# Zero rows under the low-part score pass and the Fourier tail of a two-layer encoder, with three scratch tiles merged

## The chip, the cores and the metric

One Trainium2 chip, one of its cores. The metric is the device time of one execution in microseconds, the median of several runs. The engines named below are TensorE (PE in the rows, its weight loads PEld), VectorE (DVE), ScalarE (ACT), GpSimd (POOL) and SyncE (SP, which issues most DMAs).

## What is computed

Two layers over 1040 positions (1024 and 16 meta tokens) of width 1024, all in float32:

```python
for li in range(DEPTH):                       # 2
    h = rms_norm(h_res, norm_gain[li])
    f_in, q, k, v, gate = split(h @ w_in[li])
    f_out = fourier_mixer(f_in, w_fourier[li])   # Re(FFT2 over positions, 128 channels), 4 groups, linear map
    q, k = rotary(rms_norm(q)), rotary(rms_norm(k))   # 4 heads x 2 maps x 64
    p = softmax(q k^T / 8)                     # two maps per head
    o = rms_norm((p[0] - lam * p[1]) @ v) * (1 - lambda_init)
    h_res = h_res + (concat(f_out, o) * silu(gate)) @ w_out[li]
return h_res[:, 16:]
```

## The kernel before

**Products in three passes.** Every large matrix product is made of float32r parts: each operand is split in a high and a low part, and high by high, high by low and low by high are added up in PSUM. TensorE takes at most 512 columns in a matmul, and the operands' rows (the contracted dimension) are the partitions, up to 128 of them.

**Order of work.** A layer has a Fourier part (`fourier`), the projection of head 0 (`head_projection`), attention (`attention`) and the output projection. The projections of heads 1 to 3 and the Fourier half of the output projection are a generator that `fill(n)` advances by some steps, of three matmuls of 512 columns each, between the steps of attention. The order on each engine is fixed when the program is built: a planner simulates the program's timeline and puts each instruction where its inputs and buffers are ready by its own reckoning, with priorities for what frees a PSUM bank. At run time each engine takes its instructions in that order.

**Attention.** A head's queries are handled in groups of two token tiles of 128 rows (in layer 0 the last group also has the 16 meta rows). One tile of one group is an item: 36 items in layer 0, 32 in layer 1. `scores` (line 620) handles an item in two passes, one for each of the two maps c. A pass takes the one large PSUM tile S (three banks), and makes three matmuls of 264, 512 and 264 columns with the high part of the queries against 128 rows, 64 of high and 64 of low keys (line 630), then three more with the low part of the queries against the 64 rows of high keys (line 632). VectorE finds the row maximum and copies S out (line 637), ScalarE takes the exponential (line 640). After both passes VectorE joins the two maps (line 648). One item later `drain` transposes the result in eight and one matmuls (`transposes`, lines 658 and 665), and after the last tile of a group `values` multiplies it with the values (lines 677 and 678, the latter with 80 rows). `finish` (line 683) is called in the gap after the first score pass of the second item of the next group: it transposes the group's output `osb` into a PSUM bank `pb` (line 691), copies it to `ot` (693), squares it on ScalarE for the norm, with the squares going to the scratch tile `sqo` and only the sum used (699), and multiplies with the gate (706).

**Queries.** `build_queries` (line 602) makes for each group `qa` and `qb`, each with 128 rows, and one `ql` whose upper and lower 64 rows are the low parts for the two maps. A pass of `scores` reads the half of `ql` and the half of the keys that belong to its map.

**Banks.** PSUM has the tile S, two banks G for the projections (`gbank`) and three banks M (`bank`) that are handed out in turn to transposes, keys, queries, values, `finish` and the Fourier transform.

**Fourier part.** `transform` (line 358) is called four times in a layer, for one channel group each: it folds 1040 positions to four sequences of about 260, of which 256 are multiplied with tables in `tab` (line 391, six matmuls for each sequence) and the remaining 4 or 5 are packed with their low parts into 48 rows of `tl`, transposed to `ut` and multiplied with the 48-row table `tabt` (line 393, one matmul for each sequence). That is 16 matmuls of line 393 in a layer. Both tables are loaded by DMA from GpSimd's queue (lines 317 and 319).

**Head projection.** For each token tile 24 matmuls of 512 columns (line 546), then `evacuate`: ScalarE makes the gate's tanh in `thg` (line 479, one buffer), VectorE the gate in `gs` (481, two buffers), which SyncE writes to DRAM (487); ScalarE copies the rest out of the bank (482 to 485). Scratch tiles under the tag `sq` have three buffers of 288 columns, which `rope_tables` and `small_constants` use as well.

Of the kernel before, what the change touches and what calls it, by code (L numbers as in the profile page):

```python
# [10 lines left out]
F32 = mybir.dt.float32  # L11
# [7 lines left out]
P = 128  # L19
# [14 lines left out]

C0 = 248                                    # first score column, so that the chunks end at bank edges
CHUNKS = ((0, 264), (264, 776), (776, 1040))
# token columns of each pass of the Fourier projections, per layer
FCHUNKS = (((0, 256), (256, 640), (640, 1040)), ((384, 768), (0, 384), (768, 1040)))
HOME = "G0G1G2G0G"                          # psum bank of each token tile while head 0 is projected
# weight splits given to the vector engine: every n-th one (0: none)  # L40
SHF, SH0, SHH, SHO = 2, 4, (3, 3, 0, 2), 2
STAGE = 4                                   # token tile at which the next weights start to load
WAT, MT = 2, 6                              # token tiles after which the first weights and the meta tile come
EVAC = 600                                  # priority of what frees a psum bank
# pace of the projections that run between the steps of attention, per layer
FIRST, FILL, LAG, XHD = (8, 5), (0.96, 0.93), (7, 8), (0, 1)
KEYS = (2, 1)                               # query group from which the next head's keys are built


@with_exitstack  # L50
def trunk(ctx: ExitStack, tc, x, meta, ngain, w_in, w_f, qg, kg, lq1, lk1, lq2, lk2, subg, w_out,
# [15 lines left out]
    def nm(s):  # L67
        uid[0] += 1
        return f"{s}_{uid[0]}"
# [10 lines left out]
    def f(ap):  # L80
        return ap.bitcast(F32)

# [1 line left out]
    ident = cst.tile([P, P], F32, name="ident")  # L84
# [35 lines left out]
    def small_constants(ini):  # L120
        W = DEPTH * HD
        lv = [ini.tile([P, 288], F32, tag="sq", name=nm("lv"), bufs=3) for _ in range(2)]
        for i, v in enumerate((lq1, lk1, lq2, lk2)):
# [20 lines left out]

    def rope_tables(li, rp):
        cs = rp.tile([P, 288], F32, tag="sq", name=nm("cs"), bufs=3).rearrange("p (j t d) -> p j t d", j=2, d=ROT)
        sp.dma_start(cs, rope_d)
        gb = rp.tile([P, 288], F32, tag="sq", name=nm("gb"), bufs=3)[:, 0:64]
        gb = gb.rearrange("p (i j d) -> p i j d", i=2, j=2)
        for i, g in enumerate((qg, kg)):  # L150
            sp.dma_start(gb[:, i, 0, :], g[li, 0:ROT].partition_broadcast(P))
            sp.dma_start(gb[:, i, 1, 0:8], g[li, 8:16].partition_broadcast(P))
            sp.dma_start(gb[:, i, 1, 8:16], g[li, 0:8].partition_broadcast(P))
        for j, dst in enumerate((cgt, sgt)):
            for i in range(2):
                dve.tensor_tensor(dst[:, :, i, :], cs[:, j],
                                  gb[:, i, j, :].unsqueeze(1).to_broadcast([P, NT + 1, ROT]), op=ALU.mult)

# [1 line left out]
    class Weights:  # L160
# [50 lines left out]

# [1 line left out]
    def norm_tile(hT, hM, gb, xt, t, wk, inplace=False):  # L213
# [24 lines left out]

# [1 line left out]
    def token_tiles(li):  # L240
# [60 lines left out]

# [1 line left out]
    def fourier(li, hT, fo, ep, w, nxt):  # L303
# [10 lines left out]
        ul = fo.tile([P, 8, P], F32R, name="ul")  # L314
        ut = fo.tile([48, P], F32R, name="ut")
        tab = fo.tile([P, 4, 2, 2, NFT], F32R, name="tab")
        pool.dma_start(tab, dft_d)
        tabt = fo.tile([48, 4, NFT], F32R, name="tabt")
        pool.dma_start(tabt, dftt_d)
        ph = fo.tile([P, 4, NFT], F32R, name="ph")  # L320
# [37 lines left out]
        def transform(g, usb):  # L358
# [24 lines left out]
            pe.transpose(pb[0:48, 0:P], tl, ident)  # L383
            act.copy(ut, pb[0:48, 0:P])
            dve.tensor_tensor(ut[32:48], pb[32:48, 0:P], f(ut[32:48]), op=sub)
# [32 lines left out]
        for gp in range(2):  # L418
# [20 lines left out]
            if gp == 0:  # L439
                channel_maps()  # L440
                with tc.issue_after(ins.ins):
                    rope_tables(li, ep)
                    if li == 0:
                        small_constants(ep)
# [7 lines left out]

# [1 line left out]
    def head_projection(li, h, hT, hM, ep, wk, store, w, nxt, progress):  # L454
# [9 lines left out]
        def evacuate(t, ps, a, kv):  # L464
            nonlocal ss
            R = tile_rows(t)
            with tc.high_priority(EVAC):
                if t == NT:
                    pm = [ep.tile([P, 288], F32, tag="sq", name=nm("pm"), bufs=3) for _ in range(2)]
                    for part, u, v in ((pm[0], a, 256), (pm[1], 256, 384 if kv else 512)):  # L470
                        part = part[0:R, u % 256:(v - 1) % 256 + 1]
                        act.copy(part, ps[32:32 + R, u:v])
                        dve.tensor_tensor(part, ps[0:R, u:v], part, op=ALU.add)
                    pqk, pvg = pm[0], pm[1]
                else:
                    pqk, pvg = ps[:, 0:256], ps[:, 256:512]
                if not kv:
                    th = ep.tile([P, P], F32, tag="thg", name=nm("thg"), bufs=1)
                    act.activation(th[0:R], pvg[0:R, P:2 * P], AF.Tanh, scale=0.5)
                    gs = ep.tile([P, P], F32, tag="gs", name=nm("gs"), bufs=2)  # L480
                    dve.scalar_tensor_tensor(gs[0:R], th[0:R], 1.0, pvg[0:R, P:2 * P], op0=ALU.add, op1=ALU.mult)
                act.copy(qk[0:R, t, a:256], pqk[0:R, a:256])
                sq = ep.tile([P, 288], F32, tag="sq", name=nm("sq"), bufs=3)
                act.activation(sq[0:R, a:256], pqk[0:R, a:256], AF.Square)
                act.copy(va[0:R, t, :], pvg[0:R, 0:P])  # L485
# [9 lines left out]
            if t % 3 == 2:  # L495
# [12 lines left out]

                r1 = ep.tile([P, 288], F32, tag="sq", name=nm("r1"), bufs=3)
                r2 = ep.tile([P, 288], F32, tag="sq", name=nm("r2"), bufs=3)  # L510
                r1 = r1[:, 0:12 * ROT].rearrange("p (t c d) -> p t c d", t=6, c=2)
# [41 lines left out]

# [1 line left out]
    def attention(li, wk, store, fill, marks, ready, progress):  # L555
# [5 lines left out]
        pool.memset(f(att), 0.0)  # L561
        half = (slice(0, HD), slice(HD, P))

        def group_tiles(gi):
# [37 lines left out]
        def build_queries(h, gi):  # L602
# [8 lines left out]
            qb = wk.tile([P, 272], F32R, tag="qb", name=nm("qb"))  # L611
            ql = wk.tile([P, 272], F32R, tag="ql", name=nm("ql"))
            for dst, s, o in ((qa, half[0], half[1]), (qb, half[1], half[0])):
                act.activation(dst[s, 0:w], pb[s, 0:w], AF.Copy, scale=qgc[s, li:li + 1])
                dve.tensor_copy(dst[o, 0:w], f(dst[s, 0:w]))
                dve.scalar_tensor_tensor(ql[s, 0:w], pb[s, 0:w], qgc[s, li:li + 1], f(dst[s, 0:w]),
                                         op0=ALU.mult, op1=ALU.subtract)
            return qa, qb, ql

        def scores(keys, gq, i, t, ls, gaps):  # L620
            R = tile_rows(t)
            qo = P * i
            ql = gq[2]
            l2 = sm.tile([P, 1], F32, tag="l2", name=nm("l2"))
            pp = []
            for c in range(2):
                q, kk, s = gq[c], keys[c], half[c]
                ps = big()
                for a, b in CHUNKS:
                    pe.matmul(ps[0:R, C0 + a:C0 + b], lhsT=q[:, qo:qo + R], rhs=kk[:, a:b], start=True, stop=False)  # L630
                for a, b in CHUNKS:
                    ins = pe.matmul(ps[0:R, C0 + a:C0 + b], lhsT=ql[s, qo:qo + R], rhs=kk[s, a:b],  # L632
                                    start=False, stop=True)
# [49 lines left out]
        def finish(h, gi, osb, ls):  # L683
            sets = [(0, 2, P)] + ([(2, 1, NMETA)] if len(group_tiles(gi)) > 2 else [])
            for i0, n, R in sets:
# [4 lines left out]
                for i in range(n):  # L690
                    pe.transpose(pb[0:R, P * i:P * i + P], osb[:, P * (i0 + i):P * (i0 + i) + R], ident)
                ot = wk.tile([P, 2, P], F32, tag="ot", name=nm("ot"), bufs=1)
                act.copy(ot[0:R, 0:n], pb[0:R, 0:P * n].rearrange("p (t d) -> p t d", t=n))
                r1 = sm.tile([P, 2], F32, tag="r1", name=nm("r1"))
                dve.reciprocal(r1[0:R, 0:n], ls[0:R, i0:i0 + n])
                so = sm.tile([P, 2], F32, tag="so", name=nm("so"))
                sqo = wk.tile([P, P], F32, tag="sqo", name=nm("sqo"), bufs=1)
                for i in range(n):
                    act.activation(sqo[0:R], ot[0:R, i], AF.Square, scale=r1[0:R, i:i + 1],
                                   accum_out=so[0:R, i:i + 1])  # L700
# [63 lines left out]

# [1 line left out]
    def phase_out(li, nh, gb, wk, w, load, ready):  # L766
# [52 lines left out]

# [1 line left out]
    def open_pool(name, side=None, bufs=1):  # L821
# [175 lines left out]
```

## Time and profile before

| | |
|---|---|
| median of 3 runs | 1269.27 us (1268.62 to 1269.63) |
| span of the profiled execution | 1267.7 us |
| busy, TensorE / VectorE / ScalarE / GpSimd | 1224.9 / 838.8 / 646.9 / 258.7 us |
| granted clock of TensorE, mean share | 0.993 |
| line 630 and line 632, matmuls | 408 each |
| line 393, matmuls | 32 |
| attention stretches | about 224 to 603 and 861 to 1219 us |

The times are of one execution, the span from its first to its last instruction. A group's busy time is the time in which at least one of its instructions was under way. Matmuls are pipelined, so that each one's duration (0.28 us for 256 columns) is longer than the distance to the next start; what a matmul costs in a dense stream is read from the starts. A timeline row gives start, time until the end, engine, line and operation, output and inputs, sizes as rows\*columns of the weights and partitions x columns of the moving operand, the count that is merged in the row, and in brackets the idle time of the engine before it with what ended it. "issue" is a wait for which the profile shows no cause.

### The profile page before, as it was taken

Reading aid. Unit: us, or ns where it says so; the run is one execution under the profiler, and the core shown is the slowest. Engines: PE = TensorE matmul, PEld = TensorE weight load, DVE = VectorE, ACT = ScalarE, POOL = GpSimd, SP = SyncE. Lnnn points to the kernel's source line nnn. Section 1 sums busy time; section 2 is a strip of 40 time slices with the busy share of each in tenths; the row PEclk is TensorE's granted clock in tenths of the full one; section 3 lists DMA queues with packets and bytes.
Section 4 is the critical chain, followed back from the end, with each engine's and each line's share of the span. In section 5 each row is a group of like instructions: output and inputs, shape, how many; then the busy total and the mean of one; then the engine's idle time right before and its main releaser. Section 6 shows DMA issues by size and latency. Waiting matters only on the chain.

```text
span 1267.7 us, 18708 instructions
## 1 busy us (share of the span) xinstructions
PE 1224.9 (97%) x6676; PEld 999.5 (79%) x6676; DVE 838.8 (66%) x1793; ACT 646.9 (51%) x1588; POOL 258.7 (20%) x219
## 2 busy tenths in 40 slices
PE   6999899999999999999999999999999999999998
PEld 6999787777776776778879998877777877777786
DVE  6352435777788778888673425458687887788863
ACT  6232325566656667556453222345566676756631
POOL 5101215023112112102011103160141122211200
PEclk9999899999999999999999999999999999999999
DMA  7320203003002004643335202020020110364353
GB/s 229 121 72 34 71 26 96 7 16 87 12 23 75 15 24 151 206 151 125 129 112 169 67 18 84 28 78 26 17 80 24 46 49 24 95 212 149 108 154 117
DMA packets 103612, 105.46 MB, mean 83 GB/s; under 512 B 11232, under 2 KB 87584, under 8 KB 103264
## 3 DMA queue, kind: packets, MB, share of 16 engines
q1 hardware_dynamic: 103104, 99.59, 25.0%
q0 software_dynamic: 416, 4.70, 1.1%
q8 instruction: 52, 0.85, 0.3%
q14 instruction: 40, 0.33, 0.1%
HBM read 74.62 MB, written 29.62 MB: 82 GB/s over the span
## 4 chain that ended last, share of the span: by engine, by line
PE 75%; DVE 8%; DMA 5%; ACT 4%; issue 4%; POOL 2%; SPq 1%; POOLq 0%; ACTq 0%; DVEq 0%
PE G L546 23%; PE G L286 10%; PE G L350 6%; PE M L677 6%; PE S L350 6%; PE S L632 6%; PE S L630 4%; PE S L546 3%; PE M L658 3%; PE M L391 2%; DMA wst<-in_w_in_dram 2%; POOL wl L184 2%; DVE p L637 1%; DVE p L648 1%; PE M L402 1%
## 5 line engine op out<-in xcount | busy, mean ns | idle before, releaser
L546 PE MATMUL G<-wh,hT 128*128 128x512 f32 x896 | 313.6, 409 | 4.2 <-ACT va L485 1.8
L546 PEld LDWEIGHTS G<-wh,hT 128*128 128x128 f32 x896 | 168.1, 189 | 57.2 <-issue 16.1
L640 ACT ACTIVATE p<-p,mx 128x1040 f32<-128x1040 f32 x136 | 158.5, 1165 | 101.7 <-DVE p L637 101.1
L637 DVE TENSOR_SCALAR_CACHE_REDUCE p<-S 128x1040 f32<-128x1040 f32 x136 | 167.9, 1234 | 45.9 <-PE S L632 34.1
L546 PE MATMUL G<-wl,hT 128*128 128x512 f32 x448 | 177.6, 398 | 1.6 <-POOL wl L184 1.5
L184 POOL TENSOR_TENSOR wl<-wst,wh 128x512 fp32r<-128x512 f32 x82 | 114.4, 1405 | 254.3 <-ACT wh L182 167.3
L286 PE MATMUL G<-wh,yh 128*128 128x512 f32 (+2 forms) x276 | 109.5, 409 | 3.7 <-DVE xt L293 2.7
L286 PE MATMUL G<-wl,yh 128*128 128x512 f32 (+2 forms) x276 | 106.5, 395 | 0.0
L182 ACT CAST wh<-wst 128x512 fp32r<-128x512 f32 x128 | 74.6, 619 | 56.6 <-DMA wst<-in_w_in_dram 24.2
L632 PE MATMUL S<-k,ql 64*128 64x264 f32 (+3 forms) x408 | 99.7, 350 | 0.0
L546 PEld LDWEIGHTS G<-wl,hT 128*128 128x128 f32 x448 | 84.8, 189 | 19.0 <-POOL wl L184 3.2
L500 POOL TENSOR_TENSOR rsq<-ss,nhalf 128x12 f32<-128x12 f32 x24 | 55.0, 2292 | 218.0 <-DVE ss L498 194.1
L350 PE MATMUL G<-hT,wh 128*128 128x384 f32 (+3 forms) x384 | 96.6, 332 | 0.0
L286 PE MATMUL G<-wh,yl 128*128 128x512 f32 (+1 forms) x260 | 94.1, 402 | 0.0
L663 DVE TENSOR_TENSOR atl<-M,ath 128x512 fp32r<-128x512 f32 x136 | 86.5, 656 | 9.6 <-ACT ath L662 8.5
L350 PE MATMUL S<-hT,wh 128*128 128x256 f32 (+3 forms) x384 | 91.4, 321 | 1.0 <-DVE sg L438 1.0
L648 DVE SCALAR_TENSOR_TENSOR p<-p,cc,p 128x1040 f32<-128x1040 f32 (+1 forms) x68 | 90.2, 1327 | 1.4
L662 ACT CAST ath<-M 128x512 fp32r<-128x512 f32 x136 | 73.0, 562 | 23.5 <-PE M L658 22.8
L632 PEld LDWEIGHTS S<-k,ql 64*128 64x128 f32 (+1 forms) x408 | 55.0, 179 | 35.1 <-issue 34.2
L184 DVE TENSOR_TENSOR wl<-wst,wh 128x512 fp32r<-128x512 f32 x46 | 46.6, 1017 | 43.5 <-ACT wh L182 43.4
L658 PE MATMUL M<-ident,p 128*128 128x128 f32 x544 | 73.5, 271 | 0.9 <-DVE atl L663 0.4
L703 POOL TENSOR_TENSOR rso<-so,nhalf 128x2 f32<-128x2 f32 (+1 forms) x36 | 26.8, 746 | 229.3 <-DVE so L701 223.5
(190 smaller groups left out, 2554.5 us busy)
## 6 DMA issues: line engine op xcount, KB each, us to landing
wst<-in_w_in_dram SPq DMA_DIRECT2D x64, 192.0 KB, 2.8
xt<-in_x_dram SPq DMA_DIRECT2D x16, 512.0 KB, 4.2
wst<-in_w_in_dram SPq DMA_DIRECT2D x32, 256.0 KB, 3.6
wst<-in_w_out_dram SPq DMA_DIRECT2D x16, 512.0 KB, 4.0
xmid<-xt SPq DMA_DIRECT2D x16, 512.0 KB, 3.3
xt<-xmid SPq DMA_DIRECT2D x16, 512.0 KB, 4.4
tab<-in_dft_dram POOLq DMA_DIRECT2D x2, 2096.0 KB, 10.6
yfd<-sg SPq DMA_DIRECT2D x8, 520.0 KB, 2.7
```

What stands on the lines that cost most here:

```text
L182: act.copy(h, self.staged[q][:, j, :])
L184: eng.tensor_tensor(l, self.staged[q][:, j, :], f(h), op=ALU.subtract)
L286: pe.matmul(pb[0:m, 0:e - c], lhsT=a[:, k, 0:m], rhs=b[2 * k + n][:, c:e], start=k == 0 and i == 0, stop=k == 3 and i == n_pass - 1)
L350: pe.matmul(o, lhsT=w[k][:, c:c + P], rhs=hT[:, k, s, a:b], start=k == 0 and i == 0, stop=k == KT - 1 and i == 2)
L546: pe.matmul(pss[t][0:part.shape[-1], a:b], lhsT=part, rhs=w[k][:, a:b], start=k == 0 and i == 0, stop=k == KT - 1 and i == len(pairs) - 1)
L632: ins = pe.matmul(ps[0:R, C0 + a:C0 + b], lhsT=ql[s, qo:qo + R], rhs=kk[s, a:b], start=False, stop=True)
L637: dve.tensor_scalar(pc[0:R], ps[0:R, C0:C0 + L], -1.0, None, op0=ALU.mult, op1=ALU.min, accum_out=mx[0:R])
L640: act.activation(pc[0:R], pc[0:R], AF.Exp, bias=mx[0:R], scale=-1.0, accum_out=lc)
L648: dve.scalar_tensor_tensor(pp[0][0:R], pp[1][0:R], cc[0:R], pp[0][0:R], op0=ALU.mult, op1=ALU.add)
L658: pe.transpose(pb[:, R * j:R * j + R], pa[0:R, P * kt:P * kt + P], ident[0:R, 0:R])
L663: dve.tensor_tensor(atl[:, 4 * c:4 * c + 4, qo:qo + R], src, f(hi), op=ALU.subtract)
L677: pe.matmul(po[:, 0:w], lhsT=v[:, kt, :], rhs=a[:, kt, 0:w], start=kt == 0 and i == 0, stop=False)
```

## The change

The low part of the queries gets four tiles of its own that live as long as `attention`, two for each map, with zeros written once in the 64 rows that the map doesn't use; the matmuls of line 632 take all 128 rows of them and of the keys. `ut` and `tabt` get 128 rows, zeroed before their 48 rows are filled, and line 393 takes all of them. `thg` is merged into `gs`, `ot` into the first 256 columns of `osb`, and the squares go back to the PSUM bank `pb` in place of `sqo`. `cs` of the rotary tables leaves the tag `sq` for a tile of its own in the Fourier part's pool, and the other tiles under `sq` become 256 columns wide. The rest of the diff takes comments away.

```diff
-        cs = rp.tile([P, 288], F32, tag="sq", name=nm("cs"), bufs=3).rearrange("p (j t d) -> p j t d", j=2, d=ROT)
+        cs = rc.tile([P, 288], F32, name=nm("cs")).rearrange("p (j t d) -> p j t d", j=2, d=ROT)
...
-        ut = fo.tile([48, P], F32R, name="ut")
+        ut = fo.tile([P, P], F32R, name="ut")
+        pool.memset(f(ut), 0.0)
         tab = fo.tile([P, 4, 2, 2, NFT], F32R, name="tab")
         pool.dma_start(tab, dft_d)
-        tabt = fo.tile([48, 4, NFT], F32R, name="tabt")
-        pool.dma_start(tabt, dftt_d)
+        tabt = fo.tile([P, 4, NFT], F32R, name="tabt")
+        pool.memset(f(tabt), 0.0)
+        pool.dma_start(tabt[0:48], dftt_d)
...
-            act.copy(ut, pb[0:48, 0:P])
+            act.copy(ut[0:48], pb[0:48, 0:P])
...
-                    th = ep.tile([P, P], F32, tag="thg", name=nm("thg"), bufs=1)
-                    act.activation(th[0:R], pvg[0:R, P:2 * P], AF.Tanh, scale=0.5)
                     gs = ep.tile([P, P], F32, tag="gs", name=nm("gs"), bufs=2)
-                    dve.scalar_tensor_tensor(gs[0:R], th[0:R], 1.0, pvg[0:R, P:2 * P], op0=ALU.add, op1=ALU.mult)
+                    act.activation(gs[0:R], pvg[0:R, P:2 * P], AF.Tanh, scale=0.5)
+                    dve.scalar_tensor_tensor(gs[0:R], gs[0:R], 1.0, pvg[0:R, P:2 * P], op0=ALU.add, op1=ALU.mult)
...
+        qlow = [[wk.tile([P, 272], F32R, name=f"ql{n}{c}", bufs=1) for c in range(2)] for n in range(2)]
+        for pair in qlow:
+            for c in range(2):
+                pool.memset(f(pair[c][half[1 - c]]), 0.0)
...
-            ql = wk.tile([P, 272], F32R, tag="ql", name=nm("ql"))
-            for dst, s, o in ((qa, half[0], half[1]), (qb, half[1], half[0])):
+            low = qlow[gi % 2]
+            for dst, ql, s, o in ((qa, low[0], half[0], half[1]), (qb, low[1], half[1], half[0])):
...
-                    ins = pe.matmul(ps[0:R, C0 + a:C0 + b], lhsT=ql[s, qo:qo + R], rhs=kk[s, a:b],
+                    ins = pe.matmul(ps[0:R, C0 + a:C0 + b], lhsT=ql[:, qo:qo + R], rhs=kk[:, a:b],
                                     start=False, stop=True)
...
-                ot = wk.tile([P, 2, P], F32, tag="ot", name=nm("ot"), bufs=1)
+                ot = osb[:, 0:2 * P].rearrange("p (t d) -> p t d", t=2)
...
-                sqo = wk.tile([P, P], F32, tag="sqo", name=nm("sqo"), bufs=1)
                 for i in range(n):
-                    act.activation(sqo[0:R], ot[0:R, i], AF.Square, scale=r1[0:R, i:i + 1],
+                    act.activation(pb[0:R, P * i:P * i + P], ot[0:R, i], AF.Square, scale=r1[0:R, i:i + 1],
                                    accum_out=so[0:R, i:i + 1])
```

## Rows read from the trace of the kernel before

**Rows 1.** The page: busy time by engine, then the chain's shares.

```profile
PE 1224.9 (97%) x6676; PEld 999.5 (79%) x6676; DVE 838.8 (66%) x1793; ACT 646.9 (51%) x1588; POOL 258.7 (20%) x219
...
PE 75%; DVE 8%; DMA 5%; ACT 4%; issue 4%; POOL 2%; SPq 1%; POOLq 0%; ACTq 0%; DVEq 0%
```

**Rows 2.** Attention stretches: length, busy PE, PEld, DVE, ACT, POOL, clock, DMA.

```profile
224.00:603.00 379.00, 369.85 (x1999) 283.81 (x1998) 300.80 (x664) 238.79 (x584) 70.25 (x59) 1.00 0.24 75
861.00:1219.00 358.00, 353.15 (x1924) 279.07 (x1922) 288.29 (x609) 220.51 (x535) 69.06 (x54) 1.00 0.25 78
```

**Rows 3.** Timeline of TensorE's matmuls around one score pass.

```profile
401.92 0.29 PE L630 MATMUL S<-k,qb 128*128 128x264 f32 x1
402.04 0.28 PE L678 MATMUL M<-att,vt 80*128 80x256 f32 x1
402.16 0.52 PE L630 MATMUL S<-k,qb 128*128 128x512 f32 x2
402.61 0.74 PE L632 MATMUL S<-k,ql 64*128 64x264 f32 x3
403.27 0.50 PE L546 MATMUL G<-wh,hT 128*128 128x512 f32 x1
403.61 0.39 PE L546 MATMUL G<-wl,hT 128*128 128x512 f32 x1
403.84 0.63 PE L546 MATMUL G<-wh,hT 128*128 128x512 f32 x2
```

**Rows 4.** Timeline of TensorE's weight loads around the same pass.

```profile
402.04 0.31 PEld L630 LDWEIGHTS S<-k,qb 128*128 128x128 f32 x2
402.61 0.41 PEld L632 LDWEIGHTS S<-k,ql 64*128 64x128 f32 x3 [0.25 <-issue]
```

**Rows 5.** Line 632: weight loads (ns min/median/max), idle time before it (us, times).

```profile
L632 PEld LDWEIGHTS S<-k,ql x408: 88/185/188, 225.1 to 1218.8; 64*128 64x128 f32 x128, 64*16 64x16 f32 x8
...
  issue: 34.2, 133
```

**Rows 6.** Timeline around a matmul of line 393; then that line's count.

```profile
84.76 0.28 PE L391 MATMUL M<-tab,ul 128*128 128x262 f32 x1
84.97 0.38 PE L393 MATMUL M<-tabt,ut 48*128 48x262 f32 x1
85.28 0.51 PE L391 MATMUL M<-tab,uh 128*128 128x260 f32 x2
85.62 0.28 PE L391 MATMUL M<-tab,ul 128*128 128x260 f32 x1
...
L393 PE MATMUL M<-tabt,ut x32: 381/382/387, 85.0 to 825.6; 48*128 48x262 f32 x16, 48*128 48x260 f32 x16
```

**Rows 7.** Stretches from item to item, as rows 2: first and last of 66.

```profile
224.50:231.50 7.00, 6.46 (x29) 4.43 (x28) 3.60 (x8) 2.64 (x6) 0.00 (x0) 1.00 0.00 0
...
1199.40:1211.40 12.00, 12.00 (x61) 9.34 (x60) 11.67 (x24) 7.42 (x19) 0.70 (x1) 1.00 0.27 81
```

**Rows 8.** Timeline around one `finish`; then waits of line 665: us, times, longest.

```profile
259.66 0.35 ACT L693 COPY ot<-M 128x256 f32<-128x256 f32 x1
...
261.79 0.40 ACT L699 ACTIVATE sqo<-ot,r 128x128 f32<-128x128 f32 x1
...
260.87 0.28 PE L665 MATMUL M<-ident,p 128*16 128x128 f32 x1
...
PE M L665 <- DVE atl L663: 4.3, 6, 1.1
```

**Rows 9.** Timeline of GpSimd as attention begins; then line 319's DMA issues.

```profile
206.31 0.33 POOL L561 MEMSET att<- 80x272 f32 x1
...
209.84 2.38 POOL L595 TENSOR_TENSOR vl<-va,vh 128x1024 fp32r<-128x1024 f32 x1 [2.95 <-ACT vh L594]
...
L319 POOL DMA_DIRECT2D tabt<-in_dftt_dram x2: 522/524/527, 38.2 to 674.2; - x2
```

**Rows 10.** Line 487, the gate's write-out: issue to landing.

```profile
DMA to landing us min/median/max: 1.3/1.5/4.1
```

More of the change, by code (lines that the diff above doesn't have):

```diff
@@ L121, in small_constants @@
         W = DEPTH * HD
-        lv = [ini.tile([P, 288], F32, tag="sq", name=nm("lv"), bufs=3) for _ in range(2)]
+        lv = [ini.tile([P, 256], F32, tag="sq", name=nm("lv"), bufs=3) for _ in range(2)]
         for i, v in enumerate((lq1, lk1, lq2, lk2)):
@@ L143, in small_constants, with rope_tables @@
                               op0=ALU.mult, op1=ALU.mult)
-    def rope_tables(li, rp):
-        cs = rp.tile([P, 288], F32, tag="sq", name=nm("cs"), bufs=3).rearrange("p (j t d) -> p j t d", j=2, d=ROT)
+    def rope_tables(li, rp, rc):
+        cs = rc.tile([P, 288], F32, name=nm("cs")).rearrange("p (j t d) -> p j t d", j=2, d=ROT)
         sp.dma_start(cs, rope_d)
-        gb = rp.tile([P, 288], F32, tag="sq", name=nm("gb"), bufs=3)[:, 0:64]
+        gb = rp.tile([P, 256], F32, tag="sq", name=nm("gb"), bufs=3)[:, 0:64]
         gb = gb.rearrange("p (i j d) -> p i j d", i=2, j=2)
@@ L441, in fourier @@
                 with tc.issue_after(ins.ins):
-                    rope_tables(li, ep)
+                    rope_tables(li, ep, fo)
                     if li == 0:
@@ L468, in evacuate @@
                 if t == NT:
-                    pm = [ep.tile([P, 288], F32, tag="sq", name=nm("pm"), bufs=3) for _ in range(2)]
+                    pm = [ep.tile([P, 256], F32, tag="sq", name=nm("pm"), bufs=3) for _ in range(2)]
                     for part, u, v in ((pm[0], a, 256), (pm[1], 256, 384 if kv else 512)):
@@ L477, in evacuate @@
                 if not kv:
-                    th = ep.tile([P, P], F32, tag="thg", name=nm("thg"), bufs=1)
-                    act.activation(th[0:R], pvg[0:R, P:2 * P], AF.Tanh, scale=0.5)
                     gs = ep.tile([P, P], F32, tag="gs", name=nm("gs"), bufs=2)
-                    dve.scalar_tensor_tensor(gs[0:R], th[0:R], 1.0, pvg[0:R, P:2 * P], op0=ALU.add, op1=ALU.mult)
+                    act.activation(gs[0:R], pvg[0:R, P:2 * P], AF.Tanh, scale=0.5)
+                    dve.scalar_tensor_tensor(gs[0:R], gs[0:R], 1.0, pvg[0:R, P:2 * P], op0=ALU.add, op1=ALU.mult)
                 act.copy(qk[0:R, t, a:256], pqk[0:R, a:256])
-                sq = ep.tile([P, 288], F32, tag="sq", name=nm("sq"), bufs=3)
+                sq = ep.tile([P, 256], F32, tag="sq", name=nm("sq"), bufs=3)
                 act.activation(sq[0:R, a:256], pqk[0:R, a:256], AF.Square)
@@ L507, in tab @@
                     return y.unsqueeze(2).to_broadcast([P, 6, 2, hi - lo])
-                r1 = ep.tile([P, 288], F32, tag="sq", name=nm("r1"), bufs=3)
-                r2 = ep.tile([P, 288], F32, tag="sq", name=nm("r2"), bufs=3)
+                r1 = ep.tile([P, 256], F32, tag="sq", name=nm("r1"), bufs=3)
+                r2 = ep.tile([P, 256], F32, tag="sq", name=nm("r2"), bufs=3)
                 r1 = r1[:, 0:12 * ROT].rearrange("p (t c d) -> p t c d", t=6, c=2)
@@ L617, in build_queries @@
                                          op0=ALU.mult, op1=ALU.subtract)
-            return qa, qb, ql
+            return (qa, qb), low
         def scores(keys, gq, i, t, ls, gaps):
@@ L622, in scores @@
             qo = P * i
-            ql = gq[2]
             l2 = sm.tile([P, 1], F32, tag="l2", name=nm("l2"))
@@ L626, in scores @@
             for c in range(2):
-                q, kk, s = gq[c], keys[c], half[c]
+                q, ql, kk = gq[0][c], gq[1][c], keys[c]
                 ps = big()
```

## The prediction

> **What bounds the kernel now.** I read four views in this order: the engines' busy shares, the chain of work that ended last, busy time by stretch, and the order of starts on TensorE around the lines that the change touches.
>
> The busy shares and the chain say the same [rows 1]: TensorE is busy for 97% of the span and is 75% of the chain; VectorE stands at 66% and 8%. In the two attention stretches the picture is closer [rows 2]: in 379 us TensorE is busy for 369.85 and VectorE for 300.80, in 358 us 353.15 and 288.29. So TensorE runs out of work for only 9.15 + 4.85 = 14 us of 737, and VectorE is at 80%. Whatever shortens TensorE's stream there shortens the kernel, until VectorE is the later of the two.
>
> A busy TensorE is not one at its peak, so I read the starts. In the stream around a score pass [rows 3] a matmul of 256 or 264 columns with 128 rows starts 0.12 us before the next (401.92 to 402.04), one of 512 columns 0.23 us (403.61 to 403.84). The 80-row matmul of line 678 costs no more (402.04 to 402.16). The three 64-row matmuls of line 632 are another matter: from the second matmul of line 630 at 402.16 to the second of line 546 at 403.61 six matmuls start, three of 512 and three of 264 columns. At the plain spacing that is 3 x 0.23 + 3 x 0.12 = 1.05 us; it took 1.45. The weight loads say where the 0.40 lies [rows 4]: the loads of line 630 begin as the matmul before them begins, but the first load of line 632 begins at 402.61 together with its own matmul, after 0.25 us in which the load side waited for nothing that the trace shows. The matmul of line 546 that leaves the 64-row group at 403.27 takes 0.34 to its successor where 0.23 is plain. So entering and leaving a 64-row group each costs a pause and an exposed load. This wait for "issue" stands before line 632 133 times [rows 5], once for nearly each of the 408 / 3 = 136 passes.
>
> The 48-row matmul of line 393 shows the same [rows 6]: from 84.76 to 85.62 four matmuls of some 260 columns start, 4 x 0.12 = 0.48 us when plain, and 0.86 was needed: 0.38 too much. There are 32 of them.
>
> **The change part by part.** (1) *Score passes.* The low-part matmuls read all 128 rows; their query tile holds zeros in the other 64. Count and columns stay, and with them the streaming time; I take them to run like line 630, 128 rows from tiles of the same kind: 0.12, 0.23, 0.12. Each pass then loses its 0.40: the mean over entry from line 630 and exit to whatever follows, so I take 0.39 for the few passes whose neighbours are short transposes. 136 x 0.39 = 53.0 us, all on TensorE in the attention stretches.
>
> (2) *Fourier tail.* 32 x 0.38 = 12.2 us by the same reasoning, between transforms and projections, where VectorE has room. The chains in which weights are split there start at a matmul that releases their buffers, so they move forward with TensorE. Bounds: 12.2 or, if the first half of layer 0's sixteen only lengthens its wait for weights, 12.2 - 8 x 0.38 = 9.2. I take 12.2.
>
> Gross: 65.2 us.
>
> (3) *What VectorE takes back.* I cut the two attention stretches at the starts of the score items, 66 windows of together 728.4 us, the first and the last of them in [rows 7], and took 0.8 us (two passes) from the length of each. In 13 of the 66 VectorE's busy time is then more than the window, by 4.1 us in all; the last row is one: 11.67 us of work against 12.00 - 0.80 = 11.20. That is the least that is lost, if in each window the work could be packed without a gap. If all 22 windows in which VectorE would be at 95% or more gave back their whole 0.8, it would be 17.6. I take 13 x 0.8 = 10.4, the windows that are surely full, since both engines work in a fixed order and a window that overflows is not repaired by its neighbour.
>
> (4) *Squares written into PSUM (line 699).* The scratch tile goes, the output lands in the bank pb that the transposes of line 691 filled. ScalarE's own time for 128 columns changes little and it has the room; the bank is what counts. Until now it is free when line 693 has copied it, after the change only when the second square is done. In [rows 8] that is 259.66 + 0.35 = 260.01 against 261.79 + 0.40 = 262.19, 2.18 us more, 36 times. Banks of this pool are handed out in turn, three of them: finish, two sets of transposes at line 658, then line 665 gets finish's bank again. Line 665 started at 260.87, so with the old order of the engines it would hold TensorE up to 1.3 us, and all that is queued behind it (line 546's stream). The planner puts line 665 where its bank is free by its reckoning, so most of this goes. Below nothing it can't be, nothing is made earlier. Upper end 36 x 1.3 = 47; lower end 0. The nearest row is line 665's present wait for a bank, 4.3 us over 68 of them, and I take the same rate for 36: 2.3 us.
>
> (5) *Memsets.* Four of 64 x 272 at the start of attention per layer, at most 0.33 us each by the one of 80 x 272 [rows 9], 1.3 us on GpSimd. They are queued where GpSimd then waits 2.95 us for ScalarE before line 595: nothing, or 1.3 us per layer if that wait goes. The tables' memset of 1048 columns, by columns some 4 times that row, delays one DMA and what GpSimd has behind it by about 1.3 us; the DMA is issued at 38.2 [rows 9] and line 393 begins at 85.0 [rows 6]. Nothing.
>
> (6) *thg into gs, ot into osb, cs and the narrower sq tiles.* ScalarE's tanh now waits for the gate's write-out of two tiles before, which lands 1.3 to 4.1 us after its issue [rows 10]; between two token tiles lie at least 24 matmuls x 0.23 = 5.5 us. Behind such a wait the copies of lines 482 to 485 and the exponentials would be queued; the price is nothing as long as the write-out is issued in time. osb is now held until line 706 has read it; the next group writes it two items later, about 22 us at 728.4 / 66 = 11.0 us an item. Nothing.
>
> Sum: 65.2 - 10.4 - 2.3 = 52.5 us. The profiled span is 1267.7 us, 1.6 below the median of 1269.27, which I count as what lies around it: 1267.7 - 52.5 + 1.6 = 1216.8 us.
>
> **The rivals.**
> *VectorE or the banks take back half.* For it: 80% busy in the stretches, 13 full windows. Against it: 14 us of TensorE idle now. With 17.6 us for VectorE and 15 for the banks, 32.6 remain: 1237 us.
>
> *Nothing changes.* The pause would belong to the tile or the line and not to the row count. Against it: 64 rows and 48 rows, different lines and tiles, have it; 80 rows and 128 don't [rows 3, 6]. About 1269 us.
>
> *The bank becomes the bound, and the kernel slower.* Place: line 665 behind the second square. If TensorE's order is kept or the planner's reckoning is off, each finish holds TensorE for part of 2.18 us. It decides from (65.2 - 10.4) / 36 = 1.52 us a finish on; at the full 2.18 it is 78 us and 1269.3 - 65.2 + 10.4 + 78 = 1292 us. Against it: TensorE has other work ready at nearly all times, and only 4.3 us are lost at line 665 now [rows 8].
>
> *Wide groups hide no loads.* If a 128-row load could not run beside a matmul and a 64-row one could, the 408 + 32 loads at 0.185 us [rows 5] would come out in the open: 81 us, 1350 us. The trace is against it: line 630's wide loads run beside matmuls, the first narrow one doesn't [rows 4]. The Trainium skill has this rule, on the page "TensorE: Matmul & The Clock Gate", section "The mechanism" of Part 3: weight loads overlap matmuls in flight only where the row group differs. The trace disagrees: line 630 loads ahead within one group.
>
> **How the numbers follow.** Forecast 0.86, half taken back 0.08, nothing 0.02, bank 0.03, loads 0.01. The forecast's own range: from 65.2 us with nothing lost (1204) to 65.2 - 17.6 - 15 (1237, the bank at a third of its upper end); two us below the lower end for the order, which is made anew. I give 1202 to 1236. A measurement of this kernel can tell about 0.2% (2.5 us) from no change: faster 0.94, same 0.02, slower 0.04.
>
> **What would show it.** Right: the pause before line 632 gone (34 us of "issue"), its loads starting one matmul ahead, six starts from line 630 to 546 in about 1.05 us; line 393 like line 391. VectorE's share in the attention stretches near 87%, TensorE's waits for line 637 grown to some 10 us. Step 4 wrong: more than a few us of waits of line 665 for line 699. The prediction is wrong if 128 rows stall as 64 did, if a stretch is VectorE's altogether, or if the new order of work opens gaps at stage borders.

## The result and the profile after

The changed kernel takes 1238.86 us (1237.24 to 1239.31) where the one before takes 1268.94 us beside it: a ratio of 0.9757, 95% interval 0.9741 to 0.9772. It is 30.1 us faster. The forecast was 1216.8, 52.5 us faster, and its range ended at 1236.0, 2.9 us short. The direction came out, and the mechanism of the padding; two terms of the sum didn't.

The page of the changed kernel, as [rows 1], with TensorE at 95% instead of 97% and at 66% of the chain instead of 75%:

```profile
PE 1169.6 (95%) x6676; PEld 1000.8 (81%) x6676; DVE 832.9 (67%) x1793; ACT 647.4 (52%) x1588; POOL 262.8 (21%) x231
...
PE 66%; DVE 12%; DMA 7%; ACT 6%; issue 5%; POOL 2%; SPq 1%; POOLq 0%; ACTq 0%; DVEq 0%
```

First the pauses. TensorE's timeline around a score pass and around line 395 (393 before), and the weight loads and waits of line 637 (632 before), to hold against [rows 3 to 6]:

```profile
268.88 0.64 PE L637 MATMUL S<-k,ql 128*128 128x264 f32 x3
269.35 0.39 PE L547 MATMUL G<-wh,hT 128*128 128x512 f32 x1
269.58 0.39 PE L547 MATMUL G<-wl,hT 128*128 128x512 f32 x1
```

```profile
85.42 0.28 PE L393 MATMUL M<-tab,ul 128*128 128x262 f32 x1
85.54 0.29 PE L395 MATMUL M<-tabt,ut 128*128 128x262 f32 x1
85.67 0.41 PE L393 MATMUL M<-tab,uh 128*128 128x260 f32 x2
85.91 0.28 PE L393 MATMUL M<-tab,ul 128*128 128x260 f32 x1
```

```profile
L637 PEld LDWEIGHTS S<-k,ql x408: 93/188/193, 219.2 to 1187.6; 128*128 128x128 f32 x128, 128*16 128x16 f32 x8
...
  DVE p L642: 28.4, 24
```

The three low-part matmuls need 269.35 - 268.88 = 0.47 us, 0.12 + 0.23 + 0.12, where they needed 0.66, and the matmul behind them 0.23 where it needed 0.34. Four starts around line 395 take 85.91 - 85.42 = 0.49 us where they took 0.86. Before line 637 TensorE's load side waits for nothing any more; the "issue" line with its 34.2 us is gone (the last line above is who waits for line 637). So the padding does what it says.

Then the attention stretches, as [rows 2] (window, length, busy time of PE, PEld, DVE, ACT, POOL, granted clock, DMA):

```profile
219.00:602.00 383.00, 356.50 (x2031) 292.87 (x2030) 307.39 (x673) 243.51 (x592) 71.63 (x60) 0.99 0.26 77
846.00:1188.00 342.00, 331.15 (x1927) 280.42 (x1927) 281.80 (x609) 220.86 (x538) 66.89 (x54) 1.00 0.26 81
```

Layer 1's stretch is 16 us shorter than before. Layer 0's isn't: from its first score matmul to its last it is 383 us in both kernels (the window of before ends 5 us short of that). TensorE idles for 26.50 + 10.85 = 37.3 us in them, where it was 14. What it waits for is in the list of waits, here those of the load side (us, times, longest):

```profile
PEld M L670 <- DVE atl L668: 12.6, 10, 3.4
PEld M L670 <- ACT M L703: 12.1, 9, 2.3
...
PEld S L635 <- DVE p L642: 7.7, 12, 1.7
...
PEld M L663 <- ACT M L703: 4.4, 3, 1.9
```

Line 703 is the square that now writes into the PSUM bank; lines 663 and 670 are the transposes that need the next banks. 12.1 + 4.4 = 16.5 us stand directly against it; before, TensorE waited once for the square, for 0.3 us. One of these waits in the timeline of the changed kernel:

```profile
251.63 0.35 ACT L698 COPY osb<-M 128x256 f32<-128x256 f32 x1
...
251.89 1.07 ACT L667 CAST ath<-M 128x512 fp32r<-128x512 f32 x2
...
252.84 0.39 ACT L703 ACTIVATE M<-osb,r 128x128 f32<-128x128 f32 x1
...
253.38 0.37 ACT L703 ACTIVATE M<-osb,r 128x128 f32<-128x128 f32 x1
...
253.69 0.19 ACT L703 ACTIVATION_READ_ACCUMULATOR M<-osb,r 128x1 f32 x1
253.93 0.09 PEld L670 LDWEIGHTS M<-ident,p 128*16 128x16 f32 x1 [1.74 <-ACT M L703]
253.93 0.28 PE L670 MATMUL M<-ident,p 128*16 128x128 f32 x1 [1.41 <-ACT M L703]
```

The bank was copied out by 251.98. The second square ends at 253.75, its sum is read by 253.88, and line 670 starts right behind that; all of line 547's stream, which needs no such bank, stands behind line 670 in TensorE's order. It is the place that step 4 of the prediction described.

### The profile page after: what moved, and what is told of

Its sections match the earlier page's. It is cut to its first block, busy times and chain, and to the rows that moved or that the text cites. A ratio compares the mean times of both kernels' runs of the same rounds, so it can differ in the third digit from the quotient of the medians.

```text
span 1236.9 us, 18756 instructions
## 1 busy us (share of the span) xinstructions
PE 1169.6 (95%) x6676; PEld 1000.8 (81%) x6676; DVE 832.9 (67%) x1793; ACT 647.4 (52%) x1588; POOL 262.8 (21%) x231
## 4 chain that ended last, share of the span: by engine, by line
PE 66%; DVE 12%; DMA 7%; ACT 6%; issue 5%; POOL 2%; SPq 1%; POOLq 0%; ACTq 0%; DVEq 0%
PE G L547 20%; PE G L286 10%; PE G L352 7%; PE S L352 6%; PE M L682 5%; PE S L635 4%; PE S L637 3%; PE S L547 3%; DVE p L642 3%; PE M L663 2%; PE M L393 2%; DMA wst<-in_w_in_dram 2%; ACT p L645 2%; DVE p L653 1%; DMA xt<-in_x_dram 1%
## 5 line engine op out<-in xcount | busy, mean ns | idle before, releaser
L547 PE MATMUL G<-wh,hT 128*128 128x512 f32 x896 | 308.7, 404 | 4.7 <-ACT wh L182 2.5
L501 POOL TENSOR_TENSOR rsq<-ss,nhalf 128x12 f32<-128x12 f32 x24 | 58.4, 2433 | 219.4 <-DVE ss L499 190.8
L637 PE MATMUL S<-k,ql 128*128 128x264 f32 (+3 forms) x408 | 87.3, 321 | 0.0
L707 POOL TENSOR_TENSOR rso<-so,nhalf 128x2 f32<-128x2 f32 (+1 forms) x36 | 25.3, 702 | 273.6 <-DVE so L705 256.5
L663 PEld LDWEIGHTS M<-ident,p 128*128 128x128 f32 x544 | 61.6, 140 | 15.4 <-ACT M L703 4.4
```

Source lines behind the costliest of these rows:

```text
L547: pe.matmul(pss[t][0:part.shape[-1], a:b], lhsT=part, rhs=w[k][:, a:b], start=k == 0 and i == 0, stop=k == KT - 1 and i == len(pairs) - 1)
L637: ins = pe.matmul(ps[0:R, C0 + a:C0 + b], lhsT=ql[:, qo:qo + R], rhs=kk[:, a:b], start=False, stop=True)
L663: pe.transpose(pb[:, R * j:R * j + R], pa[0:R, P * kt:P * kt + P], ident[0:R, 0:R])
```

## The experiments

Two theories at the outset. *Bank*: the new idle time of TensorE is due to the bank that is held until the second square is done. *VectorE*: TensorE has run into VectorE. (A third, *order*, is in the first expectation: the planner's new order is worse as such.) The first four kernels undo or isolate parts.

**e1: Squares back in SBUF (changed kernel).**

```diff
+                sqo = wk.tile([P, P], mybir.dt.bfloat16, tag="sqo", name=nm("sqo"), bufs=1)
...
-                    act.activation(pb[0:R, P * i:P * i + P], ot[0:R, i], AF.Square, ...
+                    act.activation(sqo[0:R], ot[0:R, i], AF.Square, ...
```

> The changed kernel, but the squares of the norm go to an SBUF scratch tile (bfloat16, since float32 doesn't fit; only their float32 sum is used) in place of the PSUM bank pb. Bank theory (the 30 us of new TensorE gaps come from the bank that is held until the second square is done): the waits of line 670 and 663 for line 703, 16.5 us on the weight-load side, go, with what follows from them; 1213 to 1224 us against 1239. VectorE theory (TensorE now runs into VectorE, at 87% of the attention stretches): nothing hangs on the bank, 1236 to 1242 us. Order theory (the planner's new order is worse as such): anything between, with the gaps at other lines.

Measured: 1222.5 us, ratio to before 0.9633 (0.9614 to 0.9652). 16.4 us of the changed kernel's time hang on where the squares go. It is the fastest whole kernel of the study. What is left before line 670, load side and matmuls together:

```profile
  DVE atl L668: 15.3, 13
  ACT osb L698: 2.0, 6
```

and in the changed kernel:

```profile
  DVE atl L668: 22.1, 16
  ACT M L703: 21.4, 17
```

**e2: Only the squares moved (kernel before).**

```diff
-                sqo = wk.tile([P, P], F32, tag="sqo", name=nm("sqo"), bufs=1)
...
-                    act.activation(sqo[0:R], ot[0:R, i], AF.Square, ...
+                    act.activation(pb[0:R, P * i:P * i + P], ot[0:R, i], AF.Square, ...
```

> The kernel before, with the one edit that the squares go to the PSUM bank pb; score passes stay at 64 rows, the tail at 48. Bank theory: slower than before, by 10 to 25 us (1279 to 1294), with waits of line 665 for line 699. VectorE theory: no difference, within 2.5 us of before.

Measured: 1286.4 us, ratio 1.0147 (1.0131 to 1.0163): 17.4 us slower than before beside it (1269.04). The same price on a kernel whose score passes still pause. The line 665 of this kernel waits for it as line 670 did:

```profile
  DVE atl L663: 18.0, 15
  ACT M L698: 14.5, 13
```

**e4: Only the Fourier tail on 128 rows (kernel before).**

```diff
-        ut = fo.tile([48, P], F32R, name="ut")
+        ut = fo.tile([P, P], F32R, name="ut")
+        pool.memset(f(ut), 0.0)
...
-        tabt = fo.tile([48, 4, NFT], F32R, name="tabt")
-        pool.dma_start(tabt, dftt_d)
+        tabt = fo.tile([P, 4, NFT], F32R, name="tabt")
+        pool.memset(f(tabt), 0.0)
+        pool.dma_start(tabt[0:48], dftt_d)
...
-            act.copy(ut, pb[0:48, 0:P])
+            act.copy(ut[0:48], pb[0:48, 0:P])
```

> The kernel before, with 128 rows with zeros in the Fourier tail only. Row-group theory: 32 x 0.38 = 12.2 us less, 1255 to 1259 us. If the gain in layer 0 only lengthens its wait for weights: 1259 to 1262. If the pause belongs to the line and not to its rows: 1269.

Measured: 1257.65 us, ratio 0.9914 (0.9894 to 0.9933). 11.4 us, close to 32 x 0.38 = 12.2.

**e5: Score passes on 64 rows again (changed kernel).**

```diff
-                    ins = pe.matmul(..., lhsT=ql[:, qo:qo + R], rhs=kk[:, a:b],
+                    ins = pe.matmul(..., lhsT=ql[half[c], qo:qo + R], rhs=kk[half[c], a:b],
```

> The changed kernel, but the low-part score matmuls read the 64 rows of their map again, from the same new tiles; tail with 128 rows and all merges stay. Row-group theory: the 53 us of the score passes come back in part. Bank theory: the merges alone cost 10 to 25 us against before and the tail gives 12, so 1267 to 1282 us. VectorE theory: merges cost nothing, 1257 us.

Measured: 1275.26 us, ratio 1.0041 (1.0023 to 1.006). That is the sum of the two kernels above: 1286.4 - 11.4 = 1275.0. The tail's gain and the squares' price add up, and thg, ot, cs and sq cost little or nothing beside them. (That the two figures meet within 0.3 us is chance: this kernel's ten runs lie between 1268.7 and 1278.5 us.) Its four compute engines run their instructions in the changed kernel's order, so the padding of the score passes doesn't move the order at all; where the squares go does.

**e6: The same, squares in SBUF.** Both edits, of e1 and of e5, on the changed kernel.

> e1 (squares in SBUF, all other edits) with the low-part score matmuls on 64 rows again. What is left against before is the tail and the merges without the squares. Theory: the other merges (thg, ot, cs, narrower sq) cost nothing and the tail gives its 11.4: 1255 to 1260 us. If ot in osb or tanh in gs holds an engine: slower than 1262. The difference to e1 (1222.5) is what 128 rows give in the score passes when the bank is out of the way: 35 us by the sum of e1 and e4, against 53 of pauses.

Measured: 1256.11 us, ratio 0.9893 (0.9866 to 0.9919), within 1.6 us of the tail alone. So the other merges are free. Against e1, which runs every instruction in the same order, it gives the score passes' part without the bank: 1256.1 - 1222.5 = 33.6 us. The attention stretches of e6, then of e1:

```profile
218.00:604.00 386.00, 377.57 (x2026) 290.19 (x2026) 305.80 (x673) 242.40 (x589) 70.79 (x60) 0.99 0.25 75
847.00:1206.00 359.00, 354.21 (x1929) 280.00 (x1928) 288.79 (x611) 221.06 (x537) 69.09 (x54) 1.00 0.25 77
```

```profile
217.00:586.00 369.00, 355.66 (x2032) 293.29 (x2031) 304.98 (x674) 241.72 (x591) 70.98 (x60) 1.00 0.26 79
831.00:1172.00 341.00, 332.20 (x1927) 281.36 (x1926) 286.12 (x610) 219.56 (x536) 68.48 (x54) 1.00 0.26 81
```

TensorE's busy time, in which the pauses are counted, falls from 731.8 to 687.9 us, by 43.9. Its idle time rises from 13.2 to 22.1, by 8.9. So 44 us of pauses go and 35 come out as shorter stretches.

**e7 and e8: Is that remainder VectorE's work?** The step that joins the two maps (1.3 us for each of 68 items) left out of e1 (e7) and of the kernel before (e8); the output is that of the first map alone.

```diff
-            dve.scalar_tensor_tensor(pp[0][0:R], pp[1][0:R], cc[0:R], pp[0][0:R], op0=ALU.mult, op1=ALU.add)
```

> e1 without the step that joins the two maps (line 653, some 68 x 1.3 us of VectorE); the output is that of the first map alone, the rest of the work stays. VectorE theory (what e1 lacks of the 65 us, about 19, was taken back by VectorE): with VectorE at some 70% the pauses' gain comes out nearly whole, so this kernel is 58 to 65 us below e8. Rival (the rest was lost to the order or to the half clock): it is some 46 us below e8, as e1 is below before.

> The kernel before without the step that joins the two maps (line 648); the output is that of the first map alone. The reference for e7. Both theories: TensorE is the bound in before with 14 us of idle time in the attention stretches, so taking VectorE's work away gives at most about that: 1255 to 1269 us.

Measured: 1224.56 us (ratio 0.9647, 0.9623 to 0.9671) and 1274.94 us (1.0043, 1.0027 to 1.0058). What was expected of e8, the same by both theories, fell: with some 90 us less work VectorE made neither kernel faster, and before even 6 us slower. The difference of the two is 50.4 us, 4 us more than with the step and less than the 58 to 65 that the VectorE theory asked for. So VectorE's load as a whole is not what takes the gain back. That TensorE waits for single steps of VectorE is not excluded: in e7 it still waits 6.1 us for line 642, where e1 has 4.0.

**e9 and e13: More and less filling work (on e1).** The pace `FILL` from (0.96, 0.93) to (1.02, 0.99), and to (0.92, 0.89).

> e1 with the pace of the filling work between the steps of attention raised from 0.96 and 0.93 to 1.02 and 0.99, so that an item whose own TensorE time fell by 0.8 us gets some 6% more of the projections. VectorE theory: an item has more TensorE work beside the same VectorE work, VectorE is last less often; 2 to 8 us below e1, 1214 to 1220 us, unless the filling work runs out before attention ends and leaves its last items bare (then 1222 to 1230).

> e1 with the pace of the filling work lowered from 0.96 and 0.93 to 0.92 and 0.89; more had cost 20 us. If an item's TensorE time must leave room for its chain over ScalarE and VectorE: 2 to 8 us faster than e1, 1214 to 1221. If any change of the pace shifts the order against the banks' turn: slower, 1225 to 1245.

Measured: 1242.97 us (0.9789, 0.9756 to 0.9821) and 1255.43 us (0.9894, 0.9865 to 0.9923). Both ways slower, by 20 and 33 us; neither expectation of e9 held, and of e13 the second came out in kind, above its range. The trace of e13 shows where about half of its 33 us lies, on the load side:

```profile
PEld M L670 <- DVE atl L668: 24.4, 13, 3.2
PEld S L635 <- DVE p L642: 12.7, 17, 2.0
```

Line 670 waits 24.4 us for a bank that line 668 has to read out, 8.7 us in e1. The pace that was set before stands in a narrow place.

**e10: Is it the hold or the write?** e1 with the squares computed from the bank and written to SBUF.

```diff
-                    act.activation(sqo[0:R], ot[0:R, i], AF.Square, ...
+                    act.activation(sqo[0:R], pb[0:R, P * i:P * i + P], AF.Square, ...
```

> e1 (squares written to SBUF), but the squares are computed from the PSUM bank pb in place of its copy ot. Nothing is written to PSUM by ScalarE, yet the bank is held until the second square is done, as in the changed kernel. Bank theory (it is the hold, not the write): 1235 to 1242 us, like the changed kernel, with waits for line 704. If the write to PSUM is what costs: 1222, like e1.

Measured: 1240.5 us, ratio 0.9772 (0.9745 to 0.9799), as the changed kernel. Nothing is written to PSUM here; the bank is only read for as long. The line 670 waits for that reader:

```profile
  ACT sqo L704: 26.8, 25
  DVE atl L668: 11.4, 11
```

**e11 and e12: Finish after the item's transposes.** In the changed kernel (e11), then in e1 (e12).

```diff
-                        (lambda: (fill(2), flush_finish()), lambda: fill(2)))
+                        (lambda: fill(2), lambda: fill(2)))
...
             transposes(pa, i, t)
             fill(3)
+            flush_finish()
...
-                flush_finish()
```

> The changed kernel, squares in PSUM, but finish is called after the item's transposes (line 670) in place of the gap before them. The bank is held as long as before, but the next three users of a bank come an item later. Bank theory: the wait of line 670 for line 703 goes, 1216 to 1228 us. If the PSUM write or the planner's order as such costs: 1236 to 1242.

> e1 with finish called after the item's transposes. Waits of line 670 for a bank (8.7 us on the load side in e1, for VectorE's line 668) go in part: 1212 to 1222 us. If those waits are VectorE's pace and not the turn of the banks: 1220 to 1226, like e1.

Measured: 1237.22 us (0.9748, 0.9723 to 0.9774) and 1238.29 us (0.9743, 0.9702 to 0.9784). The wait of line 670 for line 703 went as expected, from 21.4 us to this in the changed kernel:

```profile
  DVE atl L668: 13.5, 16
...
  ACT M L703: 0.3, 1
```

but the time didn't. A later finish costs some 16 us by itself, which the kernel with SBUF squares shows, and both expectations of e12 fell. In its attention stretches TensorE idles 32.9 us where it is 22.1 in e1, and its clock is longer at the lower level (last section); what opens the gaps is not settled. Between the two late kernels the squares' place makes no difference, 1 us.

**e14 to e16: One user of a bank less.** Line 670 and its copies left out, so that the 16 meta keys' share of the values is missing: in e1, in e6 (64-row passes, squares in SBUF) and in the changed kernel.

```diff
...
-            pb = bank()
-            ins = pe.transpose(pb[0:NMETA, 0:R], pa[0:R, SEQ:L], ident[0:R, 0:R])
             marks.append(ins.ins)
-            for o in (0, 64):
-                act.copy(att[o:o + NMETA, qo:qo + R], pb[0:NMETA, 0:R])
...
```

> e1 without line 670 and its copies: the 16 meta keys' share of the values is left out, and with it the third bank that an item's transposes take. Turn theory (what the score passes gained and e1 gave back, about 13 of 47 us, is TensorE waiting at line 670 for a bank): 43 to 48 us below e15. Rival (it is the planner's order, or the chain over ScalarE and VectorE): some 34 us below e15, as e1 is below e6.

> e6 (score passes on 64 rows, squares in SBUF) without line 670 and its copies; the reference for e14. Little TensorE time goes, 68 short transposes: 1246 to 1256 us against 1256.

> The changed kernel (squares in PSUM) without line 670 and its copies. Turn theory: with one user less between finish and the next use of its bank the hold is no longer met by line 670, at most 5 us above e14. If a held bank costs whoever takes it: 16 us above e14, as the changed kernel is above e1.

Measured: 1225.88 (0.9647, 0.961 to 0.9684), 1264.84 (0.9965, 0.994 to 0.9989) and 1219.1 us (0.9624, 0.9583 to 0.9665). The last answers for the hold: without line 670 the squares in PSUM cost nothing. That the kernel is some 7 us faster than with them in SBUF says no more: the single runs of both lie between 1218 and 1227 us. The other pair is 39.0 us apart, between the 34 of the one theory and the 43 to 48 of the other, and decides nothing: the kernel with less to do came out 9 us slower than its sibling with line 670 (1264.8 against 1256.1), for which the last section has the likely reason.

## Why the prediction was wrong

**Step 1, the pauses: right in kind, too large by 9 us.** 0.40 us a pass was read at a pass that is followed by a wide matmul, and passes with a transpose beside them were called few. In the trace of before they are 46 of 136. By the starts a pass costs 0.39 us more than its columns where a wide matmul follows (90 times), and where a transpose does 0.29 (23 times, line 665) or 0.35 (23 times): 50 us in all. The busy time fell by 43.9 us instead of 53.0, so this explains 3 of the 9; where the other 6 lie is not shown. The Trainium skill, page "TensorEngine Tiling (Array Packing)", section "Key Properties", says that a change of tiling mode drains TensorE. The trace agrees as far as the pauses stand where 64 or 48 rows meet 128 and went when all had 128.

**Step 2, the tail: right.** 11.4 us for 12.2.

**Step 3, what VectorE takes back: the size met, the reckoning not shown.** 43.9 - 33.6 = 10.3 us were given back with the bank out of the way, for 10.4 in the sum. As neither the 43.9 nor the reckoning behind the 10.4 was borne out, that is luck. The planner has no part in these 10 us, since e6 and e1 run the same instructions in the same order on TensorE, VectorE, ScalarE and GpSimd. What grew is what TensorE waits for, here in e6 and then in e1 (us, times, longest):

```profile
PE M L670 <- DVE atl L668: 4.3, 6, 1.1
...
PE S L635 <- DVE p L642: 2.4, 5, 0.6
```

```profile
PE M L670 <- DVE atl L668: 6.6, 6, 1.4
PE S L635 <- DVE p L642: 4.0, 7, 0.8
```

By the same list TensorE's idle time in the attention stretches rises from 10.0 to 15.9 us behind steps of VectorE and from 2.6 to 5.5 behind steps of ScalarE. So for the larger part it is VectorE, but by single steps that TensorE reaches sooner, not by full windows: its share of the stretches came to 83% in e1 and not to 87%, and taking away some 90 us of its work gave only 4 us more (e7, e8). Whether the windows that the prediction counted are the ones that overflowed is not shown.

**Step 4, the bank: the step that failed.** The place, the hold of about 2 us and the engine that it stops were in the prediction; its price was put at 2.3 us of an upper end of 47, by the rate at which line 665 waited for a bank before [rows 8]. It measured 16.4 us (e1), 17.4 alone (e2). Nearly all of it falls in layer 0: its stretch is 383 us with the squares in PSUM and 369 without (e1), layer 1's 342 and 341; why, is not shown. The rate was the wrong row: before, the bank was free by the time that line 665 came round, so its old waits say nothing of a bank that is held 2.18 us longer. The row to go by was the other one, line 665 at 260.87 against the second square's end at 262.19, 1.3 us, which is 47 us for 36 times; about a third came true. I had also counted on the planner to move line 670 out of the way; it stayed at the head of TensorE's queue, directly behind a score pass 21 times for 23 in e1. Three runs say that it is the hold: reading the bank costs as much as writing it (e10), and with the next user of a bank later (e11 against e12) or gone (e16 against e14) the squares in PSUM cost nothing.

**Steps 5 and 6: right.** The four memsets run in GpSimd's gap before the values:

```profile
201.02 1.41 POOL L568 MEMSET ql<- 64x272 f32 x4
202.38 0.30 POOL L463 MEMSET qk<- 128x256 f32 x1
204.18 2.38 POOL L601 TENSOR_TENSOR vl<-va,vh 128x1024 fp32r<-128x1024 f32 x1 [1.49 <-ACT vh L600]
```

The wait for ScalarE before line 601 is 1.49 us where it was 2.95 [rows 9]; the memsets' 1.41 us make up the difference, and the wait wasn't used up. The merges cost nothing (e6 against e4).

**The sum again.** From before over e4, e6 and e1 to the changed kernel the steps are 11.4 + 1.5 + 33.6 - 16.4 = 30.1 us. They add up to the measured gain by construction, so the sum proves nothing; it says what each part is worth when the edits are taken in this order. Of the 22.4 us that the forecast promised too much, 14.1 are the bank's and 9.1 the passes'; the rest, 0.8 of the tail and 1.5 the other way between e4 and e6, nearly cancels.

**The rivals.** The half taken back, put at 0.08 and 1237 us, is the time that came out. Its 15 us for the banks met 16.4; its 17.6 for VectorE didn't come, but 10.3 that were given back and 9 that the passes never had. So its time is right in part by luck. The slower side didn't come: 16.4 us over 36 finishes are 0.46 us each, and 1.52 were needed. That 128-row loads would come out in the open is refuted in the trace:

```profile
251.76 0.43 PEld L637 LDWEIGHTS S<-k,ql 128*128 128x128 f32 x3
251.88 0.64 PE L637 MATMUL S<-k,ql 128*128 128x264 f32 x3
```

The load begins 0.12 us ahead of its matmul, while the one before is still streaming. The rule of the Trainium skill that the prediction weighed ("TensorE: Matmul & The Clock Gate", section "The mechanism" of Part 3) doesn't hold in these traces when it is taken alone. The same section of the Trainium skill lets a load run ahead in a second case as well, into the background weight buffer; the trace agrees with that as far as loads of the same row group run ahead, and doesn't show the buffer.

## What to carry to other kernels

A matmul of 64 or 48 rows, or a group of three, amid a stream of 128-row ones costs 0.3 to 0.4 us more than its columns, about half going in and half coming out, and one of 80 rows nothing; zero rows are cheaper than the narrow form as long as someone has room for the memset. Look twice before you save a scratch tile by writing what nobody reads into a PSUM bank: the bank is then held until that write is done, and in a fixed order the next instruction that takes a bank stops the whole engine, with all its ready work behind it. When a change lengthens a hold, take the distance between its new end and the next taker's start as the upper end of its price, of which a third came true here, and don't go by how seldom that taker waited so far. And compare the clocks before you put a few us between two builds down to the edit.

## What else the runs showed of the chip

The clock fell behind long waits of line 670. In the changed kernel line 670 waits 3.17 us from 273.6 on, in this case for line 668, and the windows behind it read (length, busy PE, PEld, DVE, ACT, POOL, clock):

```profile
270.00:276.90 6.90, 3.73 (x25) 2.65 (x23) 5.55 (x8) 5.57 (x13) 3.75 (x3) 1.00 0.25 71
276.90:280.30 3.40, 3.40 (x9) 1.99 (x9) 2.72 (x8) 0.70 (x3) 0.69 (x1) 0.51 0.05 9
280.30:290.00 9.70, 9.70 (x64) 8.25 (x63) 6.05 (x12) 8.48 (x19) 6.28 (x5) 1.00 0.50 143
```

For 3.4 us the granted clock was about 0.5, the 1.2 GHz level of its two, after a stretch in which TensorE was busy for 3.73 of 6.90 us; the attention stretches of before stand at 1.00 [rows 2]. The only other fall in the attention stretches comes right behind a wait for the second square:

```profile
573.91 0.38 PE L670 MATMUL M<-ident,p 128*16 128x128 f32 x1 [1.97 <-ACT M L703]
```

What a fall costs is read from the starts of matmuls of 512 columns:

```profile
277.31 0.63 PE L547 MATMUL G<-wl,hM 128*16 128x512 f32 x1
277.74 0.63 PE L547 MATMUL G<-wl,hT 128*128 128x512 f32 x1
278.17 0.63 PE L547 MATMUL G<-wh,hM 128*48 128x512 f32 x1
```

They stand 0.43 us apart instead of 0.23, so that of 3.4 us some 1.6 are lost, on top of the wait itself.

Among the variants the clock moves the time by more than that. Here are the attention stretches of e15, to hold against those of e6 above:

```profile
218.00:603.00 385.00, 378.81 (x2001) 292.04 (x2000) 301.56 (x642) 225.25 (x524) 75.16 (x60) 0.98 0.26 77
846.00:1216.00 370.00, 360.54 (x1917) 286.86 (x1916) 280.50 (x584) 211.72 (x483) 69.20 (x55) 0.98 0.25 76
```

By the traces' granted clock TensorE stood at the lower level, in these stretches, for:

| kernel | us | its sibling | us |
|---|---|---|---|
| e15 | 30.7 | e6 | 6.8 |
| e14 | 27.3 | e1 | 3.4 |
| e12 | 27.3 | e1 | 3.4 |
| e13 | 34.1 | e1 | 3.4 |
| e7 | 17.1 | e1 | 3.4 |
| e8 | 13.7 | before | 0 |
| e2 | 17.1 | before | 0 |
| the changed kernel | 6.8 | e1 | 3.4 |

By the starts above 24 us more at the lower level cost about 11 us, an estimate. That is as much as the 9 us by which e15 came out slower than e6, so its lighter work didn't cost time by itself; e7 (2 us), e8 (6) and e14 (3) came out slower than their siblings by no more than the clock would cost. Between e7 and e8, and between e14 and e15, it differs by 3.4 us only, so those differences stand. Runs of one kernel, whose order of work is the same, differ by it too: those of e15 go from 1257.98 us at a mean granted clock of 0.990 to 1270.47 at 0.983. For the bank the clock adds less than 2 of 16.4 us in the changed kernel, and perhaps 8 of 17.4 in e2. Why the clock falls so much oftener in e15 than in e6 is not shown.

And the square itself was no slower into PSUM than into SBUF, 0.37 us against 0.40 [rows 8].
